# Gate blocks of both mixing layers made ahead of them, for both sequences at once, by seven block products

## The chip, the cores and the metric

One core of a Trainium2 chip runs the whole kernel. The metric is device time in microseconds. The profile names the engines PE (TensorE, matrix products), PEld (its weight loads), DVE (VectorE), ACT (ScalarE), POOL (GpSimd) and SP (SyncE, which issues nearly all DMAs).

## The reference, cut to what matters

Two sequences of 512 tokens with 1024 features (`x_prompt`, `x_sample`) pass through the same encoder layer; nothing is shared between them but the weights.

```python
def encoder_layer(x, ...):
    x = x + 0.5 * swiglu(rms_norm(x, ffn1_norm), ffn1_w_gate, ffn1_w_up, ffn1_w_down)
    h = rms_norm(x, mix_norm)
    proj = h @ w_in
    aq, ak, av, mq, mk, mv, gate_pre, o_pre, g_att, g_mlstm = jnp.split(proj, split_at, axis=-1)
    aq = apply_rope(rms_norm(aq..., q_norm), cos, sin)
    ak = apply_rope(rms_norm(ak..., k_norm), cos, sin)
    att = gqa_block_attention(aq, ak, av)
    mem = mlstm_bidirectional(mq, mk, mv, gate_pre, mlstm_gate_bias, o_pre, mlstm_head_norm)
    merged = jax.nn.sigmoid(g_att) * (att @ w_up_att) + jax.nn.sigmoid(g_mlstm) * (mem @ w_up_mlstm)
    x = x + merged @ w_out
    x = x + 0.5 * swiglu(rms_norm(x, ffn2_norm), ffn2_w_gate, ffn2_w_up, ffn2_w_down)
    return x
```

`g_att` and `g_mlstm` are 1024 columns of `proj` each. The change concerns these two. They depend on `h` and `w_in` alone, not on the attention or the memory that they gate.

## The kernel before

**Numbers.** Products are made in fp32 by splitting each operand into a high and a low half (`high` is a copy to fp32r on ACT, `low` the difference on DVE) and adding three products, high x high, high x low, low x high. A block of 128 output columns for one sequence over 1024 features is therefore 8 x 3 = 24 matmuls of 128 x 512.

**Stages.** First FFN up, first FFN down, mixing layer of sequence 0, mixing layer of sequence 1, second FFN up, second FFN down. The FFNs treat both sequences together: weight and activations are cut into halves, 2 x 2 blocks each, and seven block products with sums of blocks on both sides replace eight (`B11`, `B21`, `B22`, `T1` to `T4`; the operands of the activations are the tiles `xc`). One product for a block of 128 columns is 4 x 3 = 12 matmuls. `gu_first` makes `B11` and `B21`, which need only sequence 0's columns; `gu_rest` makes the other five, which need both sequences and sums of weight halves made by DVE from the gate and the up weights (`gu_left_b`). The two column blocks that share one seven-product group are one of gate and one of up.

**The mixing layer** (`mix`, line 882, called once for each sequence) treats one sequence. Its input is `nhl[s]`, the normalised columns as high and low tiles. For sequence 0, `turn0` (line 1977) makes them while the first FFN's last products run: a transpose on TensorE, then `emit_hl` (line 145), which takes the high half with the gain on ACT and the low half on DVE straight from PSUM. For sequence 1, `fetch_rows` loads and scales the rows at the end of the first mixing layer, and `turned_next` with `each1` transposes and splits them. In `mix`, in order of the text:

- keys, values and the small gates (`kv`), then the queries (`q`), by `token_blocks` (L872), which has the tokens on the output's partitions;
- for the second sequence the first one's output projection (`out`), carried over;
- `keys`, `rotate`: norm, rotation, transposes;
- `mem_qk`, `att_gate`, `out_gate`: 128-column blocks by `block` and `unit` (L843). `att_gate` (line 1188) makes 8 blocks, takes the tanh from PSUM on ACT (L1191) into the tile `mg`;
- `attend`: eight heads of scores (L1211), peaks (DVE, L1216), exponentials (ACT, L1223), transposes (L1235), products (L1250);
- `maxima` (L1314, L1319) for the memory's stabilisers, `values` of the memory, `up_att` with `merge_att`, which multiplies by `mg`;
- `memory`: four heads, with transposes (L1485), products (L1500) and a chain of normalisation to the split columns `mem`;
- `mem_gate` (line 1557): 8 blocks again, tanh (L1563) into two-column tiles `ths`;
- `up_mem` with `merge_mem`; then for sequence 1 the output projection and squares (`last`).

After the layers `begin` (line 2088) makes `B11` and `B21` of the second FFN's first seven blocks, storing each product to DRAM (`kept`) from a ring of two rows, while `sums` makes the other five operands.

**What sets the order.** All work of the mixing layers and of `begin` and `sums` is handed to a planner (`Plan`, line 710). Each task has an engine, an estimated length, tasks it waits for, and slots it takes and gives back (`mm`, `o`, `ps`, `pt` are PSUM banks, `w` and `wr` weight tiles, `A` the big tiles, `prob`, `turn`, `f2` rows). It runs the tasks against its own clocks and emits each engine's instructions in that order; the hardware then keeps this order, each instruction waiting only for its semaphores. Among the tasks that could start, the lowest rank goes first. The block products have rank `FILL` = 5, behind all attention and memory work: TensorE makes them when nothing more urgent is ready. The table `RANK` (line 699) moves single kinds of task up or down.

Of the kernel before, what the change touches and what calls it, by code (L numbers as in the profile page):

```python
# [8 lines left out]
F32 = mybir.dt.float32  # L9
# [7 lines left out]
P = 128  # L17
S = 512
# [8 lines left out]
def encoder(ctx, tc, I, outs):  # L27
# [116 lines left out]

    def emit_hl(src, g, k, xh, xl):
        i1 = nc.scalar.activation(xh[:, k, :], src, AF.Copy, scale=g[:, k:k + 1])
        i2 = nc.vector.scalar_tensor_tensor(xl[:, k, :], src, g[:, k:k + 1], f(xh[:, k, :]),
                                       op0=ALU.mult, op1=ALU.subtract)
        return i1, i2
# [524 lines left out]
    def tok_proj(xh, xl, name, N, kk, done):  # L674
# [6 lines left out]
        def comp(k0, w):  # L681
# [17 lines left out]
    RANK = {"kv ACT w_high": -9, "q ACT w_high": -7, "gates PE gate_sums": 4.78, "keys PE turn_k": 4,  # L699
            "rotate DVE by_root": 7, "rotate PE turn_q": 48, "mem_qk ACT w_high": 12.5, "mem_qk DVE w_low": -3.5,  # L700
            "att_gate SP w_fetch": 42, "att_gate PE fn": 45.5, "att_gate ACT <lambda>": -4,
            "out_gate ACT w_high": -1.5, "out_gate DVE w_low": -16, "attend PE scores": 14, "attend DVE peak": -20,
            "attend ACT exp": -13, "attend PE turn": 3.5, "attend ACT high": 1.08, "attend DVE lower": 7.5,
            "maxima PE ends": 8.5, "values ACT w_high": -2, "values PE fn": -16.5, "up_att ACT w_high": 93,
            "up_att PE fn": -1, "memory DVE fn": 7, "memory ACT left": -5.5, "memory PE turn": 3, "memory PE out": 2,
            "mem_gate ACT fn": 1, "up_mem PE fn": -0.08, "up_mem DVE s_low": 2, "out SP w_fetch": 38, "out PE fn": 5,
            "begin ACT p_high": 10, "begin ACT out": 1.5, "sums DVE <lambda>": 1, "next ACT left_a": -3,
            "next DVE left_b": -3.5}
# [76 lines left out]
    do = Plan(mm=3, o=1, pt=2, ps=2, prob=3, x=2, y=1, turn=0, f2=2, wr=4, w=0, qk=2, bx=0, A=5, kr=0)  # L785
# [46 lines left out]
    def unit(c, ready, n, cols, src, done, last=True):  # L832
# [3 lines left out]
        for k in range(n):  # L836
            for i in range(3):
# [8 lines left out]
                t = do("PE", 0.227, 0.35 + SPARE if end else 0.0, fn, [t] if t else ready, FILL, ["mm"] if first else (),  # L846
# [6 lines left out]
    def token_blocks(views, xs_, N, done, deps=(), each=None, got=()):  # L853
# [4 lines left out]
        for j, view in enumerate(views):  # L858
            c, ready = got[j] if j < len(got) else weights(view, deps, w=1024 if N == S else 544)
            new = [ready] if ready else []  # L860
            for q in range(4):
                for kl in range(2):
# [3 lines left out]
                    for i in range(3):  # L866
                        def fn(k=k, kl=kl, q=q, i=i, c=c):
                            if k == 0 and i == 0:
                                b[q] = PO() if q == 3 else MM()
                            xh, xl = xs_()  # L870
                            x_, w_ = ((xh, c["hi"]), (xh, c["lo"]), (xl, c["hi"]))[i]
                            own(nc.tensor.matmul(b[q][:, :N], x_[:, k, q * P:(q + 1) * P], w_[:, kl, :],  # L872
# [9 lines left out]
    def mix(s, before, after, x_in, start, got, more=None):  # L882

        G = {}
        xhl = lambda: nhl[s]
        xsrc = lambda k: (nhl[s][0][:, k, :], nhl[s][1][:, k, :])

        def block(view, done, deps=(), need=()):
            c, ready = weights(view, [kv_t, *deps], need)
            return unit(c, [ready, *(x_in or ())], KD, slice(0, P), xsrc, done)  # L890
# [39 lines left out]
        kv_last = token_blocks([win_t["kv"][j] for j in range(4)], xhl, 272, kv_done, start, x_in, got)  # L930
# [73 lines left out]
        token_blocks([win_t["q"][j] for j in range(4)], xhl, 512, q_done, [kv_t])  # L1004
# [149 lines left out]
        qks, ogs = {}, {}  # L1154

        def mem_qk(h, deps=()):
            do.part = "mem_qk"
            for j in range(2):
                def done(bk, t, j=j):
# [4 lines left out]
                    a = act(512, high, [t], 2)  # L1164
# [32 lines left out]
        for d in range(KD):  # L1197
            att_gate(d)
# [358 lines left out]
        def mem_gate(d):  # L1557
            do.part = "mem_gate"
            def done(bk, t):
                def fn():  # L1560
                    if d % 2 == 0:
                        ths[d // 2] = wide("f2" if d < 2 else "t2")
# [822 lines left out]
```

## Time and profile before

| | |
|---|---|
| median of 3 runs | 2068.27 us (2067.36 to 2070.47) |
| the profiled execution: its time, its span | 2066.46 us, 2064.7 us |
| granted TensorE clock, mean | 0.998 |
| busy ACT, POOL | 943.4 us (46%), 27.5 us (1%) |
| moved by DMA | 370.14 MB, mean 179 GB/s |

The span runs from the first to the last instruction. A row of a group reads: line, engine, operation, output and inputs with their shapes, count, then total busy us and mean ns of one, then the idle time of the engine just before them and what ended it. A row of waits reads: who waited, for whom, us in total, times, longest. A row of a stretch of time gives for each engine its busy us with the number of instructions, then the granted clock, the DMA engines' mean busy share and GB/s. In time order a piece reads: start, us, what, count. Matmuls overlap, so their mean duration is not what one costs. Line numbers are those of the kernel above.

### The profile page before, as it was taken

The page shows a single profiled execution, that of the slowest core. Times are in us where ns is not written, and L with a number is a line of the kernel's source. Part 1 is how long each engine was busy: PE and PEld are TensorE (multiplying, and loading weights), DVE is VectorE, ACT ScalarE, POOL GpSimd, SP SyncE. Part 2 cuts the span into 40 slices and gives each one's busy share as a digit, 9 for nine tenths or more (in the row PEclk, how much of TensorE's full clock was granted, in tenths as well). Part 3 has the DMA queues.
Part 4 walks back from the last instruction along what each step waited for, and adds up shares of the span by engine and source line. Part 5 has one row for each costly group of instructions (what it writes and reads, how often), then busy time and mean ns, then how long its engine had stood idle before and what let it go on. Part 6 is the DMA issues. An engine that isn't in the chain of part 4 may idle for free.

```text
span 2064.7 us, 26017 instructions
## 1 busy us (share of the span) xinstructions
PE 2046.1 (99%) x9466; PEld 1696.6 (82%) x9466; DVE 1540.6 (75%) x2450; ACT 943.4 (46%) x1575; POOL 27.5 (1%) x53
## 2 busy tenths in 40 slices
PE   9999999999999999999999999999999999999997
PEld 7788888888888888888888888888788888888886
DVE  7997888876796776675665757655888887686687
ACT  7544434442225478454435845445444444443224
POOL 0000000000000000000000000000000000000001
PEclk9999999999999999999999999999999999999999
DMA  9455556699754412222443132354454644379753
GB/s 340 164 191 212 184 183 220 240 370 346 255 205 143 133 42 73 74 102 90 144 146 110 32 101 82 133 195 160 145 210 160 233 161 163 127 292 396 274 199 139
DMA packets 140912, 370.14 MB, mean 179 GB/s; under 512 B 13840, under 2 KB 13856, under 8 KB 139504
## 3 DMA queue, kind: packets, MB, share of 16 engines
q1 hardware_dynamic: 139792, 366.44, 49.9%
q0 software_dynamic: 560, 1.26, 0.3%
q8 instruction: 74, 1.21, 0.2%
q10 hardware_dynamic: 432, 0.79, 0.1%
q14 instruction: 54, 0.44, 0.1%
HBM read 263.02 MB, written 105.41 MB: 178 GB/s over the span
## 4 chain that ended last, share of the span: by engine, by line
PE 95%; DVE 2%; ACT 1%; DMA 1%; issue 1%; SPq 0%; ACTq 0%; DVEq 0%
PE mm L843 19%; PE pss L296 18%; PE pst L296 11%; PE mm L296 8%; PE mm L550 8%; PE mm L872 7%; PE pst L550 4%; PE pss L550 4%; PE pso L550 3%; PE pso L872 2%; PE pss L1211 1%; PE pst L1235 1%; PE pss L1426 1%; PE mm L2103 1%; PE mm L1250 1%; PE pso L1250 1%
## 5 line engine op out<-in xcount | busy, mean ns | idle before, releaser
L296 PE MATMUL pss<-xc,w 128*128 128x512 f32 x1632 | 389.1, 389 | 0.1
L296 PEld LDWEIGHTS pss<-xc,w 128*128 128x128 f32 x1632 | 306.1, 188 | 64.2 <-DVE xc L1810 0.5
L843 PE MATMUL mm<-xh,w 128*128 128x512 f32 x896 | 292.7, 395 | 0.1
L253 ACT ACTIVATE w<-wr 128x1024 fp32r<-128x1024 f32 (+1 forms) x120 | 125.3, 1045 | 226.0 <-PE pst L296 128.5
L843 PEld LDWEIGHTS mm<-xh,w 128*128 128x128 f32 x896 | 167.1, 188 | 33.6 <-DVE Vm L809 1.0
L296 PE MATMUL mm<-xc,w 128*128 128x512 f32 x792 | 190.8, 390 | 2.5 <-DVE w L254 1.7
L825 DVE TENSOR_TENSOR w<-wr,w 128x1024 fp32r<-128x1024 f32 (+1 forms) x110 | 131.3, 1195 | 77.8 <-ACT w L822 77.1
L254 DVE TENSOR_TENSOR w<-wr,w 128x1024 fp32r<-128x1024 f32 (+1 forms) x120 | 144.6, 1206 | 58.8 <-ACT w L253 58.3
L550 PE MATMUL mm<-w,rt 128*128 128x512 f32 x792 | 185.3, 389 | 0.0
L296 PEld LDWEIGHTS mm<-xc,w 128*128 128x128 f32 x792 | 148.2, 188 | 34.8 <-DVE w L254 2.1
L843 PE MATMUL mm<-xl,w 128*128 128x512 f32 x448 | 176.1, 393 | 0.0
L550 PEld LDWEIGHTS mm<-w,rt 128*128 128x128 f32 x792 | 148.5, 188 | 30.8
L822 ACT ACTIVATE w<-wr 128x1024 fp32r<-128x1024 f32 (+1 forms) x110 | 113.2, 1035 | 65.4 <-PE pso L872 21.7
L296 PE MATMUL pst<-xc,w 128*128 128x512 f32 x528 | 127.2, 389 | 0.7 <-DVE xc L1810 0.7
L296 PE MATMUL pst<-xc,f 128*128 128x512 f32 x528 | 127.0, 389 | 0.0
L296 PEld LDWEIGHTS pst<-xc,w 128*128 128x128 f32 x528 | 99.0, 188 | 21.9 <-DVE xc L1810 1.2
L296 PEld LDWEIGHTS pst<-xc,f 128*128 128x128 f32 x528 | 99.1, 188 | 20.6
L610 ACT ACTIVATE w<-t 128x512 fp32r<-128x512 f32 x82 | 51.6, 632 | 122.2 <-PE pst L550 63.6
L610 ACT ACTIVATE w<-wr 128x512 fp32r<-128x512 f32 x72 | 44.7, 631 | 128.1 <-PE pso L550 67.7
L843 PEld LDWEIGHTS mm<-xl,w 128*128 128x128 f32 x448 | 84.2, 188 | 16.5
L550 PE MATMUL pss<-w,rt 128*128 128x512 f32 x396 | 94.4, 389 | 0.4 <-ACT w L610 0.4
L550 PE MATMUL pst<-w,rt 128*128 128x512 f32 x396 | 94.0, 389 | 0.0
(390 smaller groups left out, 3510.7 us busy)
## 6 DMA issues: line engine op xcount, KB each, us to landing
rt<-rbuf SPq DMA_DIRECT2D x154, 512.0 KB, 5.3
rbuf<-t SPq DMA_DIRECT2D x72, 512.0 KB, 3.3
wr<-in_ffn_w_gate_dram SPq DMA_DIRECT2D x60, 512.0 KB, 4.2
wr<-in_w_in_cols_dram SPq DMA_DIRECT2D x56, 512.0 KB, 3.5
wr<-in_ffn_w_up_dram SPq DMA_DIRECT2D x44, 512.0 KB, 3.5
rbuf<-f SPq DMA_DIRECT2D x30, 512.0 KB, 3.8
rbuf<-tab SPq DMA_DIRECT2D x30, 512.0 KB, 3.9
wr<-in_ffn_w_down_dram SPq DMA_DIRECT2D x48, 256.0 KB, 6.7
```

The lines of the kernel that those rows point to most:

```text
L253: pin(nc.scalar.activation(t[:, 0], src, AF.Copy))
L254: pin(V_.tensor_tensor(t[:, 1], src, f(t[:, 0]), op=ALU.subtract))
L296: pin(nc.tensor.matmul(p, a[:, k, :], xt[:, b, k, :], start=(first and k == 0 and i == 0), stop=(k == HK_ - 1 and i == 2), skip_group_chec ...
L550: nc.tensor.matmul(p, r[:, b, d * P:(d + 1) * P], u[:, a, :], start=(first and q == 0 and k == 0), stop=(q == len(us) - 1 and k == 2), ski ...
L610: nc.scalar.activation(hi, src, AF.Copy)
L822: own(nc.scalar.activation(c["hi"], c["raw"], AF.Copy))
L825: own(V_.tensor_tensor(c["lo"], c["raw"], f(c["hi"]), op=ALU.subtract))
L843: own(nc.tensor.matmul(b["p"], w_[:, k, cols], x_, start=(k == 0 and i == 0), stop=(k == n - 1 and i == 2)))
L872: own(nc.tensor.matmul(b[q][:, :N], x_[:, k, q * P:(q + 1) * P], w_[:, kl, :], start=(k == 0 and i == 0), stop=(k == KD - 1 and i == 2)))
L1211: own(nc.tensor.matmul(p, G["qT"][:, h, b * P:(b + 1) * P], G["kv"][:, h // 4 * 2 + j, :], start=(j == 0), stop=(j == 1)))
L1235: own(nc.tensor.transpose(p[:, b * P:(b + 1) * P], G["e", h, b // 2][:, b % 2, kb * P:(kb + 1) * P], ident))
L1250: own(nc.tensor.matmul(G["po", h], G["Vst"][:, kb, h // 4, :], G["t", h, kb][:, i], start=(kb == 0 and i == 0), stop=(kb == 3 and i == 1)))
```

## The change

A new stage stands between the first FFN and the mixing layers. It makes both gates of both sequences by seven products, as the FFNs do: for each of 8 column blocks the block of `g_att` takes the place of the FFN's gate weights and that of `g_mlstm` that of its up weights.

- `gates7`: `begun_block` makes `B11` and `B21` of all 8 blocks from sequence 0's columns. The first product is stored to `kept`, the tanh of their sum (sequence 0's attention gate) to `gbuf`.
- `gsums`: `sums_stage`, once the second FFN's `sums` and now a function of both, scales and transposes sequence 1's rows, makes the five other operands from both sequences' columns (sequence 0's are still in SBUF, in `grows`), and stores sequence 1's normalised columns to `xn1buf`.
- `grest`: `gates_rest` makes the five other products of each block, their sums, three tanhs, and three stores to `gbuf`.

In `mix`, `att_gate` and `mem_gate` become fetches from `gbuf`. Sequence 0 uses the tiles `xg[B11]`, `xg[B21]` as its columns; sequence 1 loads `xn1buf` (`load_next`) and splits it (`split_next`) in place of `fetch_rows` and `turned_next` with `each1`. `up_units` waits for each head's columns apart instead of for all. The second mixing layer starts on the first one's `mem_in` too. `RANK` and the counts of slots are replaced. The second FFN's `begin` uses `begun_block` as well; what it computes stays.

```diff
-    def emit_hl(src, g, k, xh, xl):
...
-    RANK = {"kv ACT w_high": -9, "q ACT w_high": -7, "gates PE gate_sums": 4.78, "keys PE turn_k": 4,
...
+    RANK = {"gates7 ACT out": -6.5, "gates7 ACT p_high": -23.5, "gsums ACT copy": 0.19, "grest ACT a_high": -1.5,
...
+            "rotate DVE by_root": 12, "rotate DVE both": -2.5, "mem_qk ACT w_high": 26, "mem_qk PE fn": 15.5,
+            "mem_qk DVE <lambda>": -22, "att_gate SP g_fetch": -17, "out_gate DVE w_low": 10, "attend DVE peak": -30,
+            "attend DVE add_o": 2.5, "attend DVE divide": 10.5, "attend ACT s_high": 4, "maxima DVE masked": 24,
+            "up_att SP w_fetch": 3, "up_att ACT w_high": 40, "up_att PE fn": 24, "up_att DVE <lambda>": -5.5,
...
-    do = Plan(mm=3, o=1, pt=2, ps=2, prob=3, x=2, y=1, turn=0, f2=2, wr=4, w=0, qk=2, bx=0, A=5, kr=0)
+    do = Plan(mm=3, o=1, pt=2, ps=2, tw=6, prob=0, x=0, y=0, turn=0, fr=2, f2=0, wr=4, w=2, qk=0, bx=0, A=4,
+              kr=0, wd=0, lone=1)
...
-        def att_gate(d):
+        def att_gate(h):
             do.part = "att_gate"
-            def done(bk, t):
-                gate_in_.append(act(512, lambda: own(nc.scalar.activation(mg()[:, d, :], bk["p"], AF.Tanh, scale=0.5)),
-                                    [t, mg_t], 2, (), ["mm"]))
-            block(win_c[12 + d], done)
+            ds = slice(h * HK_, (h + 1) * HK_)
+
+            def g_fetch():
+                nc.sync.dma_start(mg()[:, ds, :], gbuf[s][0][:, ds, :])
+            gate_in_.extend([dma(g_fetch, [mg_t, *gated_in[s][0]], 3, kb=1024)] * HK_)
...
-        up_units(0, att, att_in + v_in, merge_att)
+        up_units(0, att, [att7, *v_in], merge_att, att_in)
...
-            return block(win_c[20 + d], done, w3 if d >= 2 else v_in)
-        last_gate = [mem_gate(d) for d in range(KD)]
-        x_free = do("POOL", 0.0, 0.0, lambda: None, last_gate, 0, (), ["A", "A"])
+            def g_fetch():
+                ths[i] = wide("f2" if i == 0 else "t2")
+                nc.sync.dma_start(ths[i], gbuf[s][1][:, 2 * i:2 * i + 2, :])
+            gates_m.extend([dma(g_fetch, [*(w3 if i else v_in), *gated_in[s][1]], 3, ["prob" if i else "f2"])] * 2)
+        for i in range(KD // 2):
+            mem_gate(i)
+        x_free = do("POOL", 0.0, 0.0, lambda: None, users, 0, (), ["A", "A"])
...
-        last_w = up_units(1, mem, mem_in, merge_mem)
+        last_w = up_units(1, mem, w3, merge_mem, mem_in)
...
     def turn0(k):
         if k == 0:
-            nhl[0] = xhl_tiles()
-        emit_hl(turn_rows(xs[0].rearrange("p (h b) c -> p h b c", h=2), k, (PS, PT)[k % 2]), gm, k, *nhl[0])
+            xg[B11], xg[B21] = xc_tile(), xc_tile()
+            grows.extend(wide("t2") for _ in range(4))
+        x = grows[k // 2][:, k % 2]
+        nc.scalar.activation(x, turn_rows(xs[0].rearrange("p (h b) c -> p h b c", h=2), k, (PS, PT)[k % 2]), AF.Copy,
+                             scale=gm[:, k:k + 1])
+        put(xg[B11 if k < HK_ else B21], k % HK_, x)
...
+    def load_next(deps):
+        def fetch():
+            t = fresh[0] = A([P, KD, S], F32, "rows")
+            for h in range(2):
+                nc.sync.dma_start(t[:, h * HK_:(h + 1) * HK_], xn1buf[:, h * HK_:(h + 1) * HK_])
+        return [dma(fetch, deps, 2, ["A"], kb=2048, n=2)]
...
+    def begun_block(view, xcl, xin, ready, row, fns, store, got=None, keep=False):
...
+        for a in range(2):
+            m = (B11, B21)[a]
+            dep = [d for d in (wt, t) if d]
+            t = seven(lambda a=a: part(c["t"], a), xcl, m, b,
+                      lambda k, a=a, dep=dep: dep + ([xin[a * HK_ + k]] if xin else []), None if a else MM,
+                      () if a else ["mm"], ["w"] if a else ())
+            last = t
+
+            def out(a=a):
+                kr[a] = row()
+                own(nc.scalar.activation(kr[a], b["p"], fns[a][0], scale=fns[a][1]))
+            t = act(512, out, [t, ready], 1, ["kr"], ["mm"] if a else ())
+            ends.append(dma(lambda a=a: store(a, kr[a]), [t], 2, (), ["kr"], kb=256))
+        return c, wt, last, ends
...
+            if keep:
+                for i, o in ((x1l, k), (x1u, k + HK_)):
+                    out[i] = [dma(lambda i=i, o=o: nc.sync.dma_start(keep[:, o:o + 2, :], x(i)), cps[i], 3)]
...
+            b22 = put_in(B22, x1u, cps[x1u])
+            t1 = diff(x0l, x1l, x0l, [*cps[x1l], in_[x0l]])
+            t3 = diff(x1l, x1u, x1l, [*cps[x1u], t1, *out[x1l]])
+            t2 = diff(x1u, x1u, x0l, [b22, t3, *out[x1u]])
+            t4 = diff(x0u, x0u, x1u, [t2, in_[x0u]])
...
+    do.part = "grest"
+    def gates_rest(j):
...
+        fetched = [dma(fetch_g, begun_g[-3:-2], 3, ["wr"]), dma(fetch_u, begun_g[-3:-2], 3, ["wr"])]
+        u = dve(512, left_sums, [*fetched, g_t], 2, ["lone"], n=4)
+        wb_t = pair_of(lambda: R["g"], wb, [u])
...
+        p1 = seven(lambda: part(wb["t"], 0), xg, T2_, bank, [wb_t, *sums_g[T2_], begun_g[-1]], PS, ["ps"], (), "Y")
+        h1 = dve(512, first_u2, [p1, v_in_], 0, ["tw"])
+        p2 = seven(wd, xg, T1, bank, [a_t, *sums_g[T1], p1], PT, ["pt"], ["wd"], "Z")
+        c5 = act(512, lambda: own(nc.scalar.activation(v5(), Z(), AF.Copy)), [p2, v_in_], 0)
+        p3 = seven(lambda: part(wc["t"], 0), xg, T3, bank, [wc_t, *sums_g[T3], h1, p2], None, (), (), "Y")
...
+        for t, row, s, i in ((s2, v5, 1, 1), (s3, u2, 1, 0), (s4, v1, 0, 1)):
+            def gate(row=row):
+                own(nc.scalar.activation(row(), row(), AF.Tanh, scale=0.5))
+            t = act(512, gate, [t], 2)
+            t = dma(lambda row=row, s=s, i=i: nc.sync.dma_start(gbuf[s][i][:, j, :], row()), [t], 2, (),
+                    ["tw"] if i == 0 else (), kb=256)
...
-    outs0, _, in1 = mix(0, fetch_rows(xbuf[1], ssq1[1]), turned_next(tiles1, each1), None, (), first)
-    rows1, ends1, xn_in = mix(1, fetch_rows(x2buf[0], ssq2[0]), turned_next(tiles2, each2), in1, in1[:1], (), outs0)
+    outs0, done0, in1 = mix(0, load_next, split_next, None, rest_w[-1:], ())
+    rows1, ends1, xn_in = mix(1, fetch_rows(x2buf[0], ssq2[0]), turned_next(tiles2, each2), in1, [*in1[:1], *done0], (), outs0)
```

More of the change, by code (lines that the diff above doesn't have):

```diff
@@ new lines, in encoder, with start_gates @@
+    do.part = "gates7"
+    first = []
+    for j in range(2):
+        raw, t = fetch_w(win_c[12 + j]), w8_tile()
+        with shifted(-WEIGHTS):
+            w_pair(t, raw.rearrange("p (a k) c -> p a k c", a=2))
+        first.append({"t": t})
+    late = {}
+    def start_gates():
+        late["wd"], late["kr"] = wide("f2"), wide("f2")
+        late["k"] = Ring(late["kr"][:, i] for i in range(2))
+        late["a"] = tpool.tile([P, S], F32, tag="lone", bufs=1, name=nm("t2"))
+        grows.extend(wide("t2") for _ in range(2))
@@ L2190, in encoder @@
[L2190 to L2198 removed]
+    sums_t, _ = sums_stage(lambda: rows1["t"], ssq2[1], ends1, g2, xc, lambda i: late["up"].ring.x.rows[i], up_t,
+                           lambda o: [stored[o][0], stored[o + 1][0]], ((0, 1, 2, 3), (0, 2, 4, 3)))
```

373 lines of the change are left out of this document (220 added, 153 removed).

## The prediction

> **What bounds the kernel now.** I read the page's totals and slices first, then the chain of waits by line, then busy time per stage.
>
> ```profile
> span 2064.7 us, 26017 instructions
> PE 2046.1 (99%) x9466; PEld 1696.6 (82%) x9466; DVE 1540.6 (75%) x2450; ACT 943.4 (46%) x1575; POOL 27.5 (1%) x53
> PE   9999999999999999999999999999999999999997
> PE 95%; DVE 2%; ACT 1%; DMA 1%; issue 1%; SPq 0%; ACTq 0%; DVEq 0%
> L843 PE MATMUL mm<-xh,w 128*128 128x512 f32 x896 | 292.7, 395 | 0.1
> L843 PE MATMUL mm<-xl,w 128*128 128x512 f32 x448 | 176.1, 393 | 0.0
> ```
>
> TensorE is the bound in every slice, and it makes 95% of the chain that ended last. The two L843 rows are `unit` on the normalised columns: 896 + 448 = 1344 = 56 x 24 matmuls, so 28 blocks for each sequence: 8 for `mem_qk`, 4 for `out_gate`, 8 for `att_gate`, 8 for `mem_gate`. They sat idle for 0.1 us together: whatever waits in the mixing layers, these blocks are what TensorE does meanwhile. The change takes 16 of the 28 away from there.
>
> A matmul's mean of 389 to 395 ns is a latency; what it costs is the pitch, which pieces of the chain in order of time show:
>
> ```profile
> 124.33 2.72 PE mm L296 x12
> 682.64 32.67 PE mm L843 x144
> 1492.31 5.44 PE pss L296 x24
> ```
>
> 2.72 / 12 = 32.67 / 144 = 0.2267 us for 512 columns. The stages (columns: PE, PEld, DVE, ACT, POOL busy us, clock, DMA share, GB/s):
>
> ```profile
> 631.00:647.00 16.00, 16.00 (x97) 13.97 (x96) 12.16 (x19) 12.19 (x27) 0.00 (x0) 1.00 0.54 185
> 682.00:809.00 127.00, 127.00 (x650) 105.40 (x649) 101.59 (x190) 87.87 (x185) 0.00 (x0) 1.00 0.22 71
> 809.00:985.00 176.00, 175.94 (x851) 146.65 (x850) 111.64 (x242) 83.63 (x159) 0.00 (x0) 1.00 0.26 91
> 1060.00:1205.00 145.00, 145.00 (x736) 120.64 (x735) 90.55 (x161) 93.33 (x207) 0.00 (x0) 1.00 0.26 84
> 1205.00:1375.00 170.00, 169.94 (x804) 140.70 (x804) 110.11 (x239) 82.48 (x149) 0.00 (x0) 1.00 0.34 116
> 1416.00:1464.00 48.00, 45.72 (x215) 37.23 (x214) 38.39 (x49) 34.85 (x49) 0.00 (x0) 1.00 0.59 188
> 100.00:150.00 50.00, 50.00 (x222) 41.37 (x221) 47.09 (x64) 21.79 (x28) 0.00 (x0) 1.00 0.48 163
> ```
>
> In order: the end of the first FFN; rotation and attention of sequence 0, then its memory and up-projections; the same two of sequence 1; the start of the second FFN; and a piece of the first FFN for comparison. Only the sixth loses TensorE time worth naming, 2.28 us.
>
> **The change, part by part.** *Matmuls.* Removed: 16 blocks x 2 sequences x 24 = 768, or 174.1 us. Added: for each of 8 column blocks seven products of 12 matmuls, which give the two gates of both sequences: 8 x 84 = 672, or 152.3 us. Difference 96 x 0.2267 = 21.8 us. The 32 transposes of sequence 1 move from `turned_next` to `sums_stage` and stay 32. `mem_qk`, `out_gate`, keys, queries and values keep their plain form.
>
> The Trainium skill (TensorE: Matmul & The Clock Gate, section Back-to-back issue gap) gives two figures for 512 columns: about 216 ns alone and about 131 ns sustained in a stream of load and multiply pairs. By them the estimate of the saving would be 20.7 or 12.6 us. The trace has neither; its 226.7 ns decides.
>
> *New stage, first half* (`gates7`, `gsums`): 8 blocks x 24 matmuls, 43.5 us of TensorE, beside which the other five operands are made. It has the shape of the stage at 1416: `begin` evacuates to a ring of two rows, each stored to DRAM before it is used again, while `sums` works.
>
> ```profile
> L2175 DVE TENSOR_TENSOR xc<-t,xc 128x1024 fp32r<-128x1024 f32 x10 | 11.9, 1220 | 0.0
> L2172 ACT ACTIVATE xc<-t 128x1024 fp32r<-128x1024 f32 x10 | 10.5, 1064 | 0.8 <-DVE t L2181 0.7
> L2181 DVE TENSOR_TENSOR t<-t,t 128x1024 f32<-128x1024 f32 x8 | 9.8, 1224 | 3.2 <-DMA t<-xnbuf 2.4 <-ACT t L2164 0.5
> L2112 ACT ACTIVATE f<-mm 128x512 f32<-128x512 f32 x14 | 8.1, 593 | 7.4 <-DMA kept<-f 4.5 <-PE mm L2103 2.9
> PE mm L2103 <- ACT f L2112: 1.7, 2, 1.0
> kept<-f SPq DMA_DIRECT2D x14, 256.0 KB, 4.1
> ```
>
> There, the evacuation on ACT stood 4.5 us behind the store of its row; behind it in ACT's queue stood the halves of `xc` and of the next weights, and TensorE lost 1.7 us to it, 2.28 in all. Seven blocks there, eight here: 2.28 x 8/7 = **2.6 us**. DVE, with the same subtractions and halves, has 38.39 of 48 us there, so it isn't the bound. Lower bound 0: sequence 0's halves now stay in SBUF, so the 2.4 us for `xnbuf` goes. Upper bound: a row's cycle is 0.59 evacuation + 0.32 issue + landing, against 5.44 us of matmuls a block; with the longest landing of a store to `kept` (next fence, 7.1) that is 8.0, 2.6 over, x 8 = 20.6. I take the row of the same shape.
>
> ```profile
> L2118 SPq DMA_DIRECT2D kept<-f x14: 319/320/406, 1420.8 to 1463.1; - x14
> DMA to landing us min/median/max: 2.8/4.2/7.1
> ```
>
> (The second row is `kept` in the first FFN, 30 to 80 us.) SP also gets four 512 KB stores of `xn1buf` here, on which two of the subtractions wait; all its transfers come to about 11.5 MB in 47 us, 245 GB/s against 188 in the stage copied.
>
> *The start of it.* `turn0` now copies each column to SBUF and splits from there: 8 more ACTIVATEs of 512. Its rows:
>
> ```profile
> L610 ACT ACTIVATE w<-wr 128x512 fp32r<-128x512 f32 x72 | 44.7, 631 | 128.1 <-PE pso L550 67.7 <-PE pst L550 41.1 <-issue 6.4
> L822 ACT ACTIVATE w<-wr 128x544 fp32r<-128x544 f32 x2 | 1.3, 658 | 0.0
> L253 ACT ACTIVATE w<-wr 128x1024 fp32r<-128x1024 f32 x116 | 122.8, 1059 | 223.5 <-PE pst L296 128.5 <-DVE wr L277 67.0 <-PE pss L296 19.8
> ```
>
> ACT has 12.19 us in the 16 from 631; 8 x 0.63 more, two weight halves of 1024 instead of four of 544 (2.1 - 2.6 = -0.5): 16.7 of 16, so **0.7 us** late, bounds 0 (the last blocks' columns are wanted 2.7 us after the first) and 1.4 (twice that).
>
> *New stage, second half* (`grest`): for each block 60 matmuls, 13.6 us, beside DVE's 4 sums, 2 lows of 1024 and one of 512, 5 adds:
>
> ```profile
> L254 DVE TENSOR_TENSOR w<-wr,w 128x1024 fp32r<-128x1024 f32 x116 | 141.8, 1223 | 54.2 <-ACT w L253 53.7
> L611 DVE TENSOR_TENSOR w<-wr,w 128x512 fp32r<-128x512 f32 x72 | 51.7, 727 | 12.2 <-ACT w L610 8.9 <-PE pst L550 2.1 <-PE pso L550 1.1
> ```
>
> 10 x 0.70 + 2 x 1.22 = 9.4 of 13.6 us, 69%. The first FFN does the same five products with DVE at 47.09 of 50 and TensorE at 50.00. SP: two fetches, a load and three stores, 2.1 MB in 13.6 us or 154 GB/s, below the 163 of that row. Stall **0**; if the cover went, the excess of DVE would show, and there is none.
>
> *Mixing layers with 16 blocks fewer.* Each stage of the table loses 8 x 24 x 0.2267 = 43.5 us of TensorE but only 8 x 1.22 = 9.8 of DVE:
>
> - 682 to 809: PE 83.5, DVE 91.8. DVE is over.
> - 809 to 985: PE 129 (the 32 transposes leave too, 8 x 0.44), DVE about 102.
> - 1060 to 1205: PE 101.5, DVE 80.8.
> - 1205 to 1375: PE 126.5, DVE 100.3.
>
> ```profile
> 967.37 0.44 PE pss L1686 x4
> ```
>
> In the first, the maxima can wait for the next stage, which has room:
>
> ```profile
> L1314 DVE TENSOR_TENSOR box<-box,tab 128x1024 f32<-128x1024 f32 x8 | 9.8, 1220 | 0.0
> L1319 DVE TENSOR_REDUCE st<-box 128x8 f32<-128x1024 f32 x8 | 9.7, 1217 | 0.0
> ```
>
> 4 x 2.44 = 9.8: DVE 82.1. At the 94% of the FFN row it takes 87.3, **3.8 us** more than TensorE has. Lower bound 0 (the first head's memory work moves too). Upper bound: DVE only as dense as now, 101.59 of 127 = 80%: 82.1 / 0.80 = 102.6, 19.1 over. I take the row at 94%, because in attention DVE's 80% is reached while TensorE never waits.
>
> *The end of each memory.* `mem_gate` covered it; now `up_att` held back and `up_mem` on three heads, which each wait for their own head, must:
>
> ```profile
> 921.33 0.68 PE mm L1500 x3
> 931.06 0.69 DVE L809 TENSOR_TENSOR mem<-box,mem 128x512 fp32r<-128x512 f32 x1
> PEld mm L872 <- DVE t L1572: 0.5, 1, 0.5
> ```
>
> From the last head's last product to its split columns 9.7 us pass. Three banks x 9 matmuls of `up_mem` give 6.1; the rest must be `up_att`'s 96 matmuls (21.8 us). Bounds 0 and 2 x 3.6 = 7.2; I take **1.0**, two waits like the 0.5 that a late DVE costs there today.
>
> *Gates back from DRAM.* Two fetches of 1024 KB and four of 512 KB a sequence, put on SP among the weight fetches; stored in a stage that ends before the layer's own matmuls begin. Nothing waits until the merges: 0; price if late below.
>
> Sum: -21.8 + 2.6 + 0.7 + 0 + 3.8 + 1.0 = -13.7. The profiled execution took 2066.46 (span 2064.7 and 1.76 around it), so 2052.8; the median of the runs is 1.81 above it: **2054.6 us**.
>
> **Rivals.** *Clean*: every cover holds, no stall is added: 2068.27 - 21.8 = 2046.5. For: 0.1 us idle at L843 today. Against: the 2.28 us of the copied stage.
>
> *Vector bound*: in sequence 0's rotation and attention DVE stays at 80%: 19.1 instead of 3.8, 2069.9; half of it 2062. For: DVE is over TensorE there. Against: 94% elsewhere.
>
> *Slower, by the two-row ring of the first half*: eight blocks wait for stores; from a landing of 4.5 us each microsecond costs 8. It undoes the gain at 6.6 us (8 x 2.1 = 16.8 in place of 2.6), is slower by 0.2% from 7.2, and 2079 at 8. For: 245 GB/s there, and 7.1 has occurred. Against: median 4.1.
>
> *Gates late*: the fetches stand behind stores in SP's queue and the merges wait, once for each type and sequence, for as long as 1024 KB take:
>
> ```profile
> rows<-xbuf SPq DMA_DIRECT2D x4, 1024.0 KB, 5.1
> ```
>
> 4 x 5.1 is 20.4 at worst, half hidden by other blocks: 2064.8. Against: DMA's share is 0.22 to 0.34 in these stages.
>
> **How the numbers follow.** Forecast (2048 to 2061) 0.58; clean 0.10; vector bound 0.16; ring 0.10; late gates 0.06. About 0.2% (4.1 us) is what a measurement can tell: faster means below 2064.1. That takes the forecast, clean, half of vector bound, 0.05 of late gates and 0.01 of the ring: 0.82. Within: 0.05 + 0.01 + 0.02 = 0.08. Slower: 0.03 + 0.07 = 0.10. The range 2046 to 2067 leaves out the upper parts of vector bound and ring and a little of clean, about 2 in 10.
>
> **What would show it.** 9370 matmuls. TensorE's idle time between the first FFN's end and the first key product near 3 us, at the evacuations with `kept` or `gbuf` as releaser (the ring, if 15 or more). `grest` without waits. In sequence 0's attention a few waits on DVE or on ACT behind it; 15 or more makes it vector bound. Around the last head's `mem` a wait of a microsecond; waits at the merges on `gbuf` transfers would be late gates. The prediction is wrong if the pitch is not 0.2267 in the new products, or if the idle time grows by over 20 us.

## The result, and the profile after

The changed kernel takes 2058.23 us (median of 4 runs, 2057.05 to 2059.15) against 2067.86 us for the kernel before beside it (2067.36 to 2070.47): ratio 0.9951, 95% interval 0.9933 to 0.9968. That is 9.6 us less, where 2054.6 us and 13.7 us less were forecast. The profiled execution is one of 2058.12 us. Its totals and the chain that ended last:

```profile
span 2056.0 us, 26145 instructions
PE 2030.5 (99%) x9370; PEld 1679.7 (82%) x9370; DVE 1599.3 (78%) x2536; ACT 966.2 (47%) x1613; POOL 27.3 (1%) x53
...
PE 92%; ACT 3%; DVE 3%; DMA 1%; issue 1%; SPq 0%; ACTq 0%; DVEq 0%
```

The 9370 matmuls are there: 96 x 0.2267 = 21.8 us are saved. The span is only 8.7 us shorter, so TensorE loses 13.1 us more than before. TensorE's share of the chain fell from 95% to 92%, and ACT and DVE took it up. Busy time per stage (columns: PE, PEld, DVE, ACT, POOL busy us, clock, DMA share, GB/s):

```profile
643.00:697.60 54.60, 52.07 (x247) 42.08 (x245) 42.36 (x55) 39.55 (x58) 0.00 (x0) 1.00 0.54 190
697.60:808.40 110.80, 110.80 (x489) 90.66 (x488) 67.78 (x89) 37.48 (x56) 0.00 (x0) 1.00 0.48 167
...
857.00:925.00 68.00, 67.81 (x368) 55.91 (x368) 65.12 (x101) 54.24 (x121) 0.00 (x0) 1.00 0.24 70
...
1406.00:1456.00 50.00, 47.32 (x219) 37.96 (x218) 38.17 (x48) 34.15 (x49) 0.00 (x0) 1.00 0.55 182
```

In order: `gates7` with `gsums`; `grest`; most of the attention of sequence 0, whose last product starts at 937.3; the start of the second FFN. Busy time hides part of a loss, because a matmul that ends late counts as busy. So I also took from the timeline, for each unbroken piece, the start of the next piece minus its own start minus its count times its pitch. Example, from the rows further down: 70 products from 666.76 end at 666.76 + 70 x 0.2267 = 682.63, the next start at 683.55, so 0.92 us are lost, where the row itself says 0.59 idle. Summed by stage, in us:

```
stage                                      before   after   growth   forecast
first 100 us (code untouched)               7.88    9.54     1.7       0
gates7, gsums and their start                 -     4.34     4.3       3.3
grest                                         -     1.07     1.1       0
sequence 0: products, rotation, attention   1.95    2.78     0.8       3.8
sequence 1: the same                        1.57    2.91     1.3       0
both memories and up-projections            2.51    5.39     2.9       1.0
start of the second FFN                     3.67    4.45     0.8       0
the rest                                    0.84    1.22     0.4       0
sum                                        18.42   31.70    13.3       8.1
```

(The spans give 13.1; the pieces of the second profile miss one matmul.)

The first line of the table is not a loss of the changed code. TensorE waits once there in both profiles, 1.70 us before and 1.78 us after; then come the same nine products, first before, then after, and the stretch of the profile after in which they lie:

```profile
82.70 2.21 PE L296 MATMUL mm<-xc,w 128*128 128x512 f32 x9
```
```profile
83.06 3.76 PE L290 MATMUL mm<-xc,w 128*128 128x512 f32 x9
...
83.40:86.80 3.40, 3.40 (x10) 2.63 (x9) 3.40 (x3) 0.25 (x1) 0.00 (x0) 0.50 0.00 0
```

The granted clock is 0.50 in that stretch, and seven of these products start 0.43 us apart instead of 0.2267: 1.5 of the 1.7 us. The profile before shows no such stretch between its first 6 us and its last 9. Several experiments below show one or more, each beginning in a wait of TensorE or within 1.4 us behind one, though not behind every wait (none behind 2.06 us at 83.7 in e1); where one lies in a stage that is compared, its share is given.

The places, first in `gates7`. Who waited for whom there, and the landing times of its stores:

```profile
ACT xc L2182 <- DVE t L2190: 6.9, 3, 3.6
ACT f L2128 <- PE mm L2100: 5.2, 3, 3.3
DVE t L2190 <- DMA xn1buf<-t: 4.0, 3, 1.6
PEld mm L2100 <- ACT f L2128: 3.3, 3, 1.5
...
PE mm L2100 <- ACT f L2128: 2.1, 3, 1.1
```
```profile
kept<-f SPq DMA_DIRECT2D x8, 256.0 KB, 2.0
xn1buf<-t SPq DMA_DIRECT2D x4, 512.0 KB, 5.6
gbuf<-f SPq DMA_DIRECT2D x7, 256.0 KB, 2.0
```

TensorE waits for evacuations (L2128), as forecast, but no evacuation waits for a store: `kept` and `gbuf` land in 2.0 us. The waits have two other makers, which the timeline shows:

```profile
679.09 1.22 DVE L2190 TENSOR_TENSOR t<-t,t 128x1024 f32<-128x1024 f32 x1 [1.49 <-DMA xn1buf<-t]
680.35 2.01 ACT L2182 ACTIVATE xc<-t 128x1024 fp32r<-128x1024 f32 x2 [3.04 <-DVE t L2190]
682.26 1.24 ACT L2128 ACTIVATE f<-mm 128x512 f32<-128x512 f32 x2
683.55 10.04 PE L2100 MATMUL mm<-xc,w 128*128 128x512 f32 x43 [0.59 <-ACT f L2128]
...
693.11 1.05 ACT L2086 ACTIVATE w<-wr 128x1024 fp32r<-128x1024 f32 x1
694.05 0.59 ACT L2128 ACTIVATE f<-mm 128x512 f32<-128x512 f32 x1
694.69 3.02 PE L2100 MATMUL mm<-xc,w 128*128 128x512 f32 x12 [1.10 <-ACT f L2128]
```

At 679 the subtraction that overwrites stored columns waits for the `xn1buf` store; on ACT the halves of its result stand ahead of the evacuation, and that one ahead of TensorE. At 694 the last block is alone: its second twelve products accumulate on the bank that the evacuation has to read first, no other block stands between, and a weight half (693.11) is ahead of the evacuation.

In sequence 0, at the step from the queries to their rotation:

```profile
845.78 10.59 PE L838 MATMUL mm<-xc,w 128*128 128x512 f32 x46
...
848.26 0.18 DVE L172 TENSOR_SCALAR rs<-ssq 128x32 f32<-128x32 f32 x1
...
856.27 0.42 DVE L1131 TENSOR_TENSOR t<-t,t 128x256 fp32r<-128x256 f32 x1
...
856.83 0.63 PE L1137 MATMUL pst<-ident,t 128*128 128x128 f32 x4 [0.46 <-DVE t L1131]
858.80 0.74 PE L1213 MATMUL pss<-kv,qT 128*128 128x512 f32 x2 [0.19 <-DVE t L1131]
```

From the root's first operation to the first turned query DVE works without a break for 8.6 us; 46 products cover it, and 0.6 + 0.7 us are missing. The same step costs 1.1 us in sequence 1, but not for the same reason: there TensorE waits 0.91 us for ACT's copy of the turned queries (L1140, at 1119.83), which stands in ACT's queue behind a table load of 1.28 us, the first exponential and a weight half of 1.05 us. And at the end of sequence 1's memory:

```profile
1338.33 2.77 PE L838 MATMUL mm<-att,w 128*128 128x512 f32 x11
...
1341.14 0.69 DVE L1381 SCALAR_TENSOR_TENSOR mg<-mg,mm 128x512 f32<-128x512 f32 x1 [1.48 <-PE mm L838]
1341.97 4.36 PE L838 MATMUL mm<-mem,w 128*128 128x512 f32 x18 [0.87 <-DVE mg L1381]
```

`up_att`'s eleven products are the last cover, and the next bank is free only after its merge (L1381): 1.15 us. No wait on a `gbuf` transfer appears in either layer.

### The profile page after: what moved, and what is told of

It reads as the page before. It is cut to its first block, busy times and chain, and to the rows that moved or that the text cites. A ratio compares the mean times of both kernels' runs of the same rounds, so it can differ in the third digit from the quotient of the medians.

```text
span 2056.0 us, 26145 instructions
## 1 busy us (share of the span) xinstructions
PE 2030.5 (99%) x9370; PEld 1679.7 (82%) x9370; DVE 1599.3 (78%) x2536; ACT 966.2 (47%) x1613; POOL 27.3 (1%) x53
## 4 chain that ended last, share of the span: by engine, by line
PE 92%; ACT 3%; DVE 3%; DMA 1%; issue 1%; SPq 0%; ACTq 0%; DVEq 0%
PE pss L290 18%; PE pst L290 12%; PE mm L838 10%; PE mm L290 9%; PE mm L544 8%; PE mm L868 7%; PE pst L544 4%; PE pss L544 4%; PE pss L2100 3%; PE pso L544 3%; PE pst L2100 2%; PE pso L868 2%; PE mm L2100 2%; PE pss L1213 1%; PE pst L1237 1%; PE pss L1429 1%
## 5 line engine op out<-in xcount | busy, mean ns | idle before, releaser
L247 ACT ACTIVATE w<-wr 128x1024 fp32r<-128x1024 f32 (+1 forms) x122 | 127.3, 1045 | 227.2 <-PE pst L290 128.1
L248 DVE TENSOR_TENSOR w<-wr,w 128x1024 fp32r<-128x1024 f32 (+1 forms) x122 | 146.8, 1205 | 63.7 <-ACT w L247 63.2
L290 PE MATMUL mm<-xc,w 128*128 128x512 f32 x792 | 192.3, 393 | 2.9 <-DVE w L248 1.8
L290 PEld LDWEIGHTS mm<-xc,w 128*128 128x128 f32 x792 | 149.4, 189 | 35.5 <-DVE w L248 2.2
L820 DVE TENSOR_TENSOR w<-wr,w 128x1024 fp32r<-128x1024 f32 (+1 forms) x80 | 93.6, 1172 | 30.0 <-ACT w L817 29.7
L817 ACT ACTIVATE w<-wr 128x1024 fp32r<-128x1024 f32 (+1 forms) x80 | 80.6, 1013 | 25.1 <-PE mm L838 6.7
L2100 PE MATMUL mm<-xc,w 128*128 128x512 f32 x360 | 86.0, 394 | 4.2 <-ACT f L2128 4.2
L544 PEld LDWEIGHTS pss<-w,rt 128*128 128x128 f32 x396 | 74.3, 188 | 16.5 <-ACT w L604 1.2
L544 PEld LDWEIGHTS pst<-w,rt 128*128 128x128 f32 x396 | 74.4, 188 | 15.4
L2100 PEld LDWEIGHTS mm<-xc,w 128*128 128x128 f32 x360 | 66.7, 188 | 20.7 <-ACT f L2128 7.2
```

The lines of the kernel that those rows point to most:

```text
L247: pin(nc.scalar.activation(t[:, 0], src, AF.Copy))
L248: pin(V_.tensor_tensor(t[:, 1], src, f(t[:, 0]), op=ALU.subtract))
L290: pin(nc.tensor.matmul(p, a[:, k, :], xt[:, b, k, :], start=(first and k == 0 and i == 0), stop=(k == HK_ - 1 and i == 2), skip_group_chec ...
L544: nc.tensor.matmul(p, r[:, b, d * P:(d + 1) * P], u[:, a, :], start=(first and q == 0 and k == 0), stop=(q == len(us) - 1 and k == 2), ski ...
L817: own(nc.scalar.activation(c["hi"], c["raw"], AF.Copy))
L820: own(V_.tensor_tensor(c["lo"], c["raw"], f(c["hi"]), op=ALU.subtract))
```

## The experiments

Losses by stage below are worked out as in the table. The first 100 us are the same instructions in every program here; TensorE lost between 7.1 and 10.7 us in them, so a difference of one profile of up to 3.6 us can come from there, and the stages are compared one by one.

**The control and three edits of the gate stage.**

> The changed kernel again, unaltered, as the control for the three that follow. 2058 us, within 1.5 us of its first median; in the first 100 us, whose code the change does not touch, TensorE lost 7.9 us in the profile of before and 9.5 us in that of after: if that difference is run to run, this profile lies somewhere between, if it belongs to the changed program, it is 9.5 again within 0.3.

2058.08 us (2055.86 to 2058.85), ratio 0.9952, interval 0.9938 to 0.9965; first 100 us 9.42, like the first profile of this program, but the two that follow lose 10.74 and 7.11 there with the same code: run to run. In four of the fourteen profiles (after, e2, e5, e9) some 1.6 us of it is a stretch at half the clock at 83 to 89 us; the rest of the spread isn't explained. `gates7` lost 3.88, sequence 0's attention stage 2.54, sequence 1's 2.94, the memories 2.72 and 2.69.

```diff
-                out[i] = [dma(lambda i=i, o=o: nc.sync.dma_start(keep[:, o:o + 2, :], x(i)), cps[i], 3)]
+                out[i] = [dma(lambda: None, cps[i], 3)]
```

> Leaves out the four stores of the second sequence's columns (xn1buf); the mixing layer reads x_sample_t in their place. The planned order of all instructions stays the same. Theory A (ScalarE's queue in the gate stage is held by the differences that wait 5.6 us for these stores): the two vector differences behind them start at once, the gaps of TensorE at 666.8 and 683.6 us (0.66 and 0.92 us) go, the stage loses about 2.8 us in place of 4.3, and the time is 1 to 1.6 us below the control. Theory B (the ring of two rows waits for kept and gbuf): less traffic lets those land a little sooner, 0 to 0.3 us. Theory C (the losses are only ScalarE's amount of work): no change.

2055.46 us (2054.91 to 2058.47), ratio 0.9944, interval 0.9931 to 0.9956. `gates7` lost 2.77 instead of 3.88, `grest` 1.25 instead of 1.09; all other touched stages stayed within 0.4. TensorE's own waits on engines in the two stages:

```profile
PE mm L2100 <- ACT f L2128: 1.1, 1, 1.1
PE pss L1690 <- ACT xs L2140: 0.3, 1, 0.3
```

The wait at 683 is gone, the one of the last block remains. Theory A holds with 1.1 us; the intervals of the two times overlap, so the verdict rests on the stage.

```diff
-        late["k"] = Ring(late["kr"][:, i] for i in range(2))
         late["a"] = tpool.tile([P, S], F32, tag="lone", bufs=1, name=nm("t2"))
+        late["k"] = Ring([late["kr"][:, 0], late["kr"][:, 1], late["a"]])
...
+    swap([v_stored[-1]], ["kr"], ["lone"])
```

> A third row for the evacuations of the gate stage (the row that the left sums use later). The prediction's step, that the two rows wait for their stores and lose 2.3 us, gives 2 us less than the control. Theory A, by which the stores of kept and gbuf land in 2.0 us and no row is ever waited for, gives the control's time within 0.7 us and the same gaps at 654, 667 and 684 us.

2064.83 us (2062.69 to 2066.96): 6.8 slower than the control, which no theory had. `gates7` lost 3.08 (0.8 less), but the change-over to `grest` 8.57:

```profile
DVE t L2263 <- DMA kept<-t: 8.3, 1, 8.3
...
PEld pss L2100 <- ACT w L2086: 3.5, 1, 3.5
PEld pss L2100 <- DVE w L2089: 3.3, 1, 3.3
...
DVE t L2190 <- DMA xn1buf<-t: 3.1, 3, 1.3
```

The borrowed row is the one in which the left sums of `grest` are formed (L2263), which now wait for its last store; the first weights of `grest` come late behind them. TensorE's own waits there are 3.0 and 2.8 us; between them and behind, from 698.6 to 705.5, the granted clock was 0.50, which is worth some 2.1 of the 8.57. For the question asked: a third row is worth 0.8 us at most, not 2, and in this run the `xn1buf` stores were waited for 0.9 us less too, so even the 0.8 need not be the row's.

```diff
-                out[i] = [dma(lambda i=i, o=o: nc.sync.dma_start(keep[:, o:o + 2, :], x(i)), cps[i], 3)]
+                out[i] = [dma(lambda i=i, o=o: nc.sync.dma_start(keep[:, o:o + 2, :], x(i)), cps[i], 3, kb=1000)]
```

> Only the planner's assumption on the four stores of xn1buf is changed, from 512 to 1000 KB, so that it plans them to land in 4.4 us rather than 3.2 us (measured: 5.6 us) and puts ScalarE's halves of the differences behind the evacuations that it now puts after them. Theory A: 0.5 to 1.5 us below the control, with the gap at 683.6 us gone. Rival: the order moves but the loss reappears at the next set of halves, control within 0.5 us.

2056.82 us (2055.67 to 2057.88), ratio 0.9947, interval 0.9934 to 0.9959: the fastest of the complete kernels, but not to be told from the control. `gates7` lost 3.92; the 1.3 us less are less than the 2.0 that its first 100 us lost less. The rival: the order moved, the loss stayed.

**VectorE in attention.** Three kernels with the same edit, for `s == 0`, `s == 1`, and in the kernel before:

```diff
-                    own(V_.tensor_tensor(t[:, 1], G["tp", h, kb], f(t[:, 0]), op=ALU.subtract))
+                    for _ in range(1 + (s == 0 and kb % 2 == 0)):
+                        own(V_.tensor_tensor(t[:, 1], G["tp", h, kb], f(t[:, 0]), op=ALU.subtract))
```

> The changed kernel with 16 of sequence 0's 32 subtractions `lower` done twice: 16 x 0.68 = 10.9 us more on VectorE, at the same places, nothing else moved. In sequence 0's attention VectorE is busy 65.1 of 68.0 us. Theory V (there VectorE sets the pace): what exceeds the 2.9 us of slack shows, 7 to 9 us above the control's 2058.1. Theory L (TensorE's small waits there come of latency and order, VectorE only looks full because work was drawn into it): under 4 us.

> The same 16 additional subtractions in sequence 1's attention, where VectorE is busy 85.3 of 103.0 us. Both theories: the slack of 17.7 us takes them, 0 to 2 us above the control.

> The kernel before the change with the same 16 additional subtractions in sequence 0's attention, where VectorE was busy 101.6 of 127.0 us over rotation and attention, and 55.1 of 69.0 us in the attention. The gate blocks cover them: 0 to 1.5 us above the kernel before. If it is 7 us or more here too, the cover that the change took away was not what kept VectorE's work hidden.

The times: 2063.54 (2062.21 to 2064.86), 2063.24 (2060.76 to 2064.84) and 2071.60 us (2069.52 to 2073.75) beside 2067.68 for the kernel before: 5.5, 5.2 and 3.9 us more. The stage with the added work lost 6.3 more (8.86), 4.9 more (7.85) and 3.6 more (5.53). Neither theory gave that: with 17.7 us of slack in e6, and with all the gate blocks present in e7, a third to a half of the 10.9 us showed, and in e5 (forecast 7 to 9, or under 4) about half. Waits in e5 and then in e7 (line numbers one higher than in the parent after the added line):

```profile
PEld mm L1253 <- DVE t L1247: 3.6, 6, 0.8
PEld pso L1253 <- DVE t L1247: 3.0, 5, 0.7
```
```profile
PEld mm L1251 <- DVE t L1245: 2.7, 6, 0.5
...
PEld pso L1251 <- DVE t L1245: 1.3, 3, 0.6
```

`lower` stands between a turned bank and the product that needs it, so each doubling makes that product late, slack or not; neither parent shows such a wait in these windows. So latency in a fixed order is the larger part. That the stage of sequence 0 pays most (6.3 against 4.9 and 3.6) may be what capacity adds, but this isn't shown: the times of e5 and e6 don't differ (5.5 and 5.2).

```diff
-                own(V_.tensor_tensor(G["mx", h], G["mx", h], mask(), op=ALU.add))
+                own(nc.gpsimd.tensor_tensor(G["mx", h], G["mx", h], mask(), op=ALU.add))
...
-                own(V_.tensor_tensor(G["em", h], G["eb", h], mask(), op=ALU.add))
+                own(nc.gpsimd.tensor_tensor(G["em", h], G["eb", h], mask(), op=ALU.add))
```

> The eight additions of the mask per sequence (1.21 us each) run on GpSimd in place of VectorE, at the same places of the planned order: 9.7 us less on VectorE for each sequence, of which about 6 lie in sequence 0's attention. Theory V: the 1.8 us that TensorE loses in that attention and part of the 0.8 us behind it go, 1 to 2 us below the control. Theory L: no change within 0.7 us. A loss of 1 us or more would say that GpSimd's additions are late for the memory's exponentials.

2064.80 us (2062.88 to 2066.50), 6.7 slower. Sequence 0's stage lost 8.83 instead of 2.54. Its timeline, POOL and DVE:

```profile
847.27 4.74 POOL L1317 TENSOR_TENSOR box<-box,tab 128x1024 f32<-128x1024 f32 x2 [24.30 <-issue]
...
847.35 2.36 DVE L159 SCALAR_TENSOR_TENSOR rs<-rs 128x32 f32<-128x32 f32 x1
849.75 2.32 DVE L160 TENSOR_TENSOR rs<-rs,rs 128x32 f32<-128x32 f32 x1
852.10 0.19 DVE L161 SCALAR_TENSOR_TENSOR rs<-rs,rs 128x32 f32<-128x32 f32 x1
```

GpSimd's additions fell on the root of the queries, and two operations of 0.19 us took 2.36 and 2.32 us, as long as one addition each. So this run did not take work off VectorE where it matters; it put 4.3 us into the very chain that has no cover (TensorE's wait for the first turned query grew from 0.46 to 4.76 us), and tells nothing of theory V. About 2 us more of that stage are the granted clock, 0.50 from 857.2 to 864.1. The memory of sequence 0 lost 2.4 us more as well, 1.4 of them in one wait on VectorE.

**What the mixing layers lose with the gate blocks, and what holds it down.** In the first of the next two, from the kernel before, both kinds of gate block become fetches:

```diff
-            block(win_c[12 + d], done)
+            def g_fetch():
+                nc.sync.dma_start(mg()[:, 4 * d:4 * d + 4, :], I["x_prompt_t"][:, 4 * d:4 * d + 4, :])
...
-            return block(win_c[20 + d], done, w3 if d >= 2 else v_in)
+                nc.sync.dma_start(ths[i], I["x_prompt_t"][:, 2 * i:2 * i + 2, :])
```

> The kernel before, with the gate blocks of the mixing layers left out: their tiles are fetched from an input that has the shape of gbuf, and nothing computes the gates. The 768 matmuls less are 174.1 us; what the time falls short of that is the cover that the mixing layers lose, in the order that was planned for before. By the prediction's terms (3.8 in sequence 0's rotation and attention, 1.0 at the memories' ends) 4.8 us: 1897.7 from a before of 2067. By the gaps of the two traces (about 1 us more in sequence 0's rotation and attention, 1.3 in sequence 1's, 1.7 and 2.1 in the memories) 6.1 us: 1899. A loss under 2 us would say that the changed kernel's new losses in the mixing layers come from elsewhere.

1967.06 us (1964.43 to 1967.55) beside 2067.34: 100.3 less where 174.1 us of matmuls left. 73.8 us of cover were lost, fifteen times the 4.8 that the prediction's terms give. By stretches of the mixing layers TensorE lost 23.7 (640 to 800 us, sequence 0 to the end of its attention), 20.5, 13.6 and 22.1 us (1120 to 1320, sequence 1's memory). Part of the stretch of sequence 0's attention, and TensorE's longest waits over both layers (640 to 1380):

```profile
680.00:760.00 80.00, 72.87 (x347) 57.26 (x345) 58.18 (x106) 43.27 (x86) 0.00 (x0) 0.98 0.26 76
```
```profile
PE pst L194 <- DVE rs L173: 7.6, 2, 3.8
PE pss L1211 <- ACT t L1223: 7.2, 16, 1.1
PE pst L1137 <- DVE t L1131: 5.7, 4, 2.1
```

No engine is full there (DVE 58.18 of 80): these are chains from engine to engine with nothing between. The clock has a share: in both layers together it was granted at 0.50 for 17.1 us, in four stretches in or behind such waits, and TensorE's instructions lost about 7 of the 73.8 us by that. The changed kernel, with the same blocks gone, lost 5 us more than before in the same layers. So it isn't the cover that was enough; the other edits to the layers and the new order of the plan took nearly 69 us out again.

```diff
-        last_w = up_units(1, mem, w3, merge_mem, mem_in)
+        last_w = up_units(1, mem, [*w3, *mem_in], merge_mem, mem_in)
```

> The changed kernel with up_mem waiting for all four heads of its memory, as before the change, so that its 9 matmuls of the first three heads on three banks (6.1 us) can't stand at the end of a memory. The prediction took them as cover: 3 to 6 us for each sequence, 6 to 12 us above the control. If the planner holds back enough of up_att's 96 matmuls in their place, the rival, it is 0 to 3 us.

2076.93 us (2075.22 to 2079.90), ratio 1.0046, interval 1.0032 to 1.0059: 18.9 over the control and slower than the kernel before. The memory stages lost 16.95 (2.72) and 10.27 (2.69). TensorE's waits at the end of sequence 0's memory, then of sequence 1's:

```profile
PE mm L838 <- ACT w L817: 6.2, 1, 6.2
PE pst L188 <- DVE rs L167: 3.1, 1, 3.1
```
```profile
PE mm L838 <- DVE w L820: 2.5, 1, 2.5
PE mm L838 <- ACT w L817: 2.4, 1, 2.4
```

The largest waits are for weights: the dependence on the heads holds back `up_mem`'s fetches and splits, not its products alone. TensorE's waits there come to 10.1 us in sequence 0 (with 0.8 more for a weight's low half) and 5.3 in sequence 1. Most of the rest is the clock, granted at 0.50 for 13.7 us in sequence 0, in and behind these waits, and for 6.8 us in sequence 1:

```profile
1041.90:1055.50 13.60, 7.17 (x16) 5.20 (x17) 9.02 (x10) 6.31 (x7) 0.00 (x0) 0.50 0.17 42
```

What TensorE executed there ran at half its pace and lost about 3.3 and 2.4 us beside the waits. So the 18.9 us are more than 2 x 6.1 for two reasons, the weights and the slow clock behind the waits.

**A better plan?** Two planner costs, set to what the trace shows, alone and together:

```diff
-        root_q = dve(32, hold("rq", lambda: rstd_cols(G["ssq"], 32, DA, own)), reds, 0, n=12)
+        root_q = dve(32, hold("rq", lambda: rstd_cols(G["ssq"], 32, DA, own)), reds, 0, n=22)
```

> Only the planner's cost of the query root is changed: 12 operations of 32 columns from 0.12 to 0.22 us each, which is their spacing in the trace (2.6 us for all, planned as 1.4). Theory: TensorE's waits at the first turned queries and scores (1.3 us in sequence 0, 1.1 in sequence 1) come of a plan that expects them 1.2 us too early; with the right cost other matmuls stand there and the time is 1 to 2.4 us below the control. Rival: there are no other matmuls to be had, or the rest of the order gets worse by as much: within 0.7 us of it.

> The costs of e4 (1000 KB for the stores of xn1buf) and of the query root together. If the two are independent, the sum of both: 2 to 3.5 us below the control, 2055 us or less.

2062.13 (2058.18 to 2069.90) and 2061.97 us (2059.61 to 2063.41): both 4 slower than the control. In e11 the stages of the two attentions lost 6.66 and 7.64 instead of 2.54 and 2.94. At 856 us of e11:

```profile
PE mm L838 <- DVE w L820: 3.4, 1, 3.4
```
```profile
849.39 1.23 DVE L1317 TENSOR_TENSOR box<-box,tab 128x1024 f32<-128x1024 f32 x1
...
851.13 1.21 DVE L1322 TENSOR_REDUCE st<-box 128x8 f32<-128x1024 f32 x1
...
857.70 1.22 DVE L820 TENSOR_TENSOR w<-wr,w 128x1024 fp32r<-128x1024 f32 x1
```

With the true cost the planner saw room on VectorE behind the root and put a mask and a maximum (2.4 us) into the chain; the next block's weight half (857.70) came after them, and TensorE, which had gone on to that block, stood for 3.4 us. In sequence 1 it was something else: VectorE and ACT stood behind a store to `x2buf` until 1172.1 (4.3 us of VectorE), and the product behind `lower` came 3.3 us late. Behind each of the two waits the granted clock was 0.50 for 3.4 us, worth 1.7 us each. Repairing one cost of the plan removed one wait and made longer ones. No version here beats the changed kernel by a measurable amount. Not tried: the changed kernel without its new ranks, so how much of the 69 us is order and how much is dependences is open, beyond the 18.9 of e10.

## Why the prediction was right, and where it was not

The sign, the range and the likeliest case held; the time came out 3.6 us above the forecast. Step by step:

- *Matmuls, -21.8*: 9370, at the forecast pitch. Right.
- *`gates7`, 2.6, and its start, 0.7*: 4.3 together (3.6 to 4.2 in the other profiles where this stage was left alone). The size was near, the mechanism wrong. The prediction took the wait of the copied stage for the ring's; here no row is waited for, and DMA moved 190 GB/s where 245 were expected. About 1.1 us is ACT's queue behind the `xn1buf` stores (e2), which the prediction named ("on which two of the subtractions wait") and did not price; 1.4 is the last block, whose two halves share a bank; most of the rest is the start, where the turned rows wait for ACT's scaling (the second row shown for e2, and a wait for the copies behind it).
- *`grest`, 0*: 1.1, near its start and without a wait of TensorE that the view lists. Nearly right: the cover holds.
- *Vector term, 3.8 in sequence 0*: 0.8 there and 1.3 in sequence 1. Too large, and in one place where there are two. The density was near: from 846 to the end of the last product at 938 VectorE is busy for 85.27 of 92.00 us, 93%, and for 65.12 of 68.00 in the part shown. What failed is "DVE is over": TensorE is busy for 91.35 us of the same stretch, because the new order puts other products there. The stretch from the end of the query products to the last attention product took 120.2 us before (682.4 to 802.6); without the 43.5 us of gate blocks it would be 76.7, and it takes 92. Of the 2.78 us lost in sequence 0, 1.3 are the latency of root and rotation, 8.6 us of VectorE that begin 2.5 us into 10.4 us of products; of the 2.91 in sequence 1, 1.1 are the copy behind ACT's queue. Neither shows in a sum of busy time; the rest are smaller pieces.
- *Ends of memories, 1.0*: 2.9. The mis-sized term: the waits were there, as the one shown on the way from `up_att`'s last products to `up_mem`'s, but more of them and in the whole stage. The upper bound of 7.2 held. But the prediction counted only the products (6.1 us a sequence) as the cover that `up_mem` on three heads gives, and forgot the weights' fetch and split that come forward with them, and the clock: e10, without that dependence by heads, is 18.9 us slower.
- *Gates back from DRAM, 0*: no wait. Right.
- *Counted as untouched*: 2.8 us of the growth of 13.3 (first 100 us 1.7, second FFN 0.8, rest 0.4). The first of them is run to run, 7.1 to 10.7, and in this pair of profiles 1.5 of the 1.7 is the stretch at half the clock: a sum made on one profiled execution carries this error. The start of the second FFN lost 3.6 to 4.7 in the changed kernel's variants, 3.67 and 2.82 in the kernel before (the second in e7), and the 4.7 (e1) hold 1.7 of a stretch at half the clock at 1440; some of that growth may be real, and its cause is open.

The terms of the touched stages sum to 10.5 where 8.1 were forecast. Of the rivals, *clean* was refuted by the losses above, the *ring* and *late gates* by the absence of their waits. *Vector bound*, 19.1 in sequence 0's attention, did not happen either, but e9 lost 23.7 in that stretch where 2 were lost before, with DVE at 73%: a loss of the size that the rival priced is real with the dependences and ranks of the kernel before, though with no engine full it is one of latency, and a small part of the clock behind the waits, rather than of VectorE's capacity.

## What to carry to other kernels

Work that covers waits isn't valued by its busy time: 174 us of gate blocks hid 74 us of waits and of slow clock behind them, and leaving them out paid only because the consumers' dependences were loosened (each head by itself, weights ahead of their data) and the order was made anew; price such a removal by its chains, not by the fullest engine. Look at what an in-place operation must wait for when a store of its tile is added, and at what stands behind it in the queue of the next engine. In a tuned plan a truer cost for one step isn't an improvement by itself; measure it. When a stage of TensorE is slower than its waits add up to, look at the granted clock in the rows of that stage before you explain the rest.

## Not expected of the hardware

While a GpSimd addition of 128 x 1024 (2.4 us alone) ran, VectorE operations of 32 columns took 2.36 and 2.32 instead of 0.19 us (e8), one for each addition. The Trainium skill (SBUF — State Buffer, section SBUF: two separate sides) says that VectorE and GpSimd share a port pair, which a VectorE operation with two inputs in SBUF and a GpSimd operation that reads SBUF hold by an exclusive lock for a whole instruction, and that the loser is blocked rather than slowed; the rows agree.
